# Variable-length attention: batches sorted by length on chip, and loops with one body per length class

## The chip, the cores and the metric

One Trainium2 chip, one of its cores. The traces show five engines, each with its own instructions, that work side by side (before the change PE is busy for 771.8 us of a span of 865.5, DVE for 562.0 and ACT for 549.9) and wait for one another: PE (TensorE, matrix multiply), DVE (VectorE), ACT (ScalarE), POOL (GpSimd) and SP (SyncE, which here issues most of the DMA transfers). The metric is the device time of one execution in microseconds. Executions of one kernel agree within about 1.3% here. A profiled execution gives a trace; "the span" is its length from first to last instruction, about 2 us less than the time.

## The reference

Self-attention over 32 batches of up to 512 rows, 8 heads of 64. Each batch has its own length between 64 and 511; rows from the length on are not attended to, and their output is zero.

```python
for b in range(32):
    n = lengths[b]
    q, k, v = split(x[b, :n] @ w_qkv)              # x is (32, 512, 512), w_qkv (512, 1536)
    scores = (q @ k.T) / 8                         # per head
    attn = softmax(scores)
    output[b, :n] = attn @ v                       # rows from n on stay zero
```

The draw is always the same. In classes of 64 rows (class c holds lengths up to 64c) there are, from class 8 down to class 2, 1, 3, 7, 5, 5, 6 and 5 batches. The mean length is about half of 512.

## The kernel before

The kernel before is straight-line code made by a tile framework: 32 times a projection stage (QK and V) followed by the attention stage of the batch before it. Lengths enter as masks only; every batch is computed at 512 rows.

```python
def stage_qkv(b):                                   # cut
    x16 = ...                                       # DVE: cast to f16
    for c in range(NC):                             # 16 PE transposes, ACT copies them out
        nc.tensor.transpose(pxt[:, t, :], x16[:, t, c*P:(c+1)*P], ident_f16)
        nc.scalar.copy(out=xT[:, c, :], in_=pxt)
    for m in range(2 * NC):                         # Q and K: 32 matmuls of 512 columns
        for c in range(NC):
            nc.tensor.matmul(pq, w_r[:, c, m*P:(m+1)*P], xT[:, c, :], ...)
        nc.vector.tensor_copy(out=qkT[:, m, :], in_=pq)
    for t in range(NT):                             # V: 16 matmuls of 512 columns
        ...
        nc.vector.tensor_scalar_mul(v_aug[:, t, :, 0:HD], pv, kmask[:, t, b:b+1])

def stage_attn(b):                                  # cut
    def emit_scores(i):                             # a pair of heads
        for kt in range(NT):
            psc = ps_s.tile([P, 2, MAXS], FP32)     # two such buffers in PSUM
            for par in range(2):                    # two heads, 64 rows each
                nc.tensor.matmul(psc[:, par, :], qkT[...], qkT[...])
            nc.scalar.activation(out=ep[:, :, kt, :], in_=psc, func=AF.Exp, scale=scale)
    def emit_av(i):
        ...                                         # 32 matmuls of 65 columns per pair, DVE divides
```

The softmax here doesn't subtract the row's maximum and nothing guards it: scores larger than these inputs give would overflow.

## Time and profile before

| | before |
|---|---|
| time, median of 8 runs (those beside the last experiments) | 867.6 us (865.5 to 868.9) |
| span of the profiled execution | 865.5 us |
| PE busy | 771.8 us, 89% |
| period of one batch | 26.0 us |

The first view is the profile's page: the line of busy times (share of the span, number of instructions), and the chain of work that ended last, as shares of the span.

```profile
PE 771.8 (89%) x7168; PEld 410.7 (47%) x7168; DVE 562.0 (65%) x1990; ACT 549.9 (64%) x645; POOL 1.1 (0%) x8
...
PE 53%; ACT 41%; issue 3%; DMA 1%; POOLq 0%; DVE 0%; ACTq 0%; POOL 0%
```

The second view is the costliest groups. The columns are line, engine, operation, tiles and shapes, count, then busy time and the mean of one in ns, then the engine's idle time just before them and what ended it.

```profile
L178 ACT ACTIVATE ep<-psc 128x1024 f16<-128x1024 f32 x512 | 482.1, 1068 | 281.6 <-PE psc L171 280.2
L171 PE MATMUL psc<-qkT 64*128 64x512 f16 x1024 | 230.0, 381 | 57.5 <-ACT ep L178 36.8
L127 PE MATMUL pq<-xT,w_r 128*128 128x512 f16 x1024 | 235.9, 384 | 6.4 <-ACT w_r L74 6.4
L188 PE MATMUL pav<-v_aug,ep 128*128 128x65 f16 x4096 | 206.2, 195 | 11.1 <-ACT ep L178 11.1
```

The third view is PE's timeline for part of one batch (start, duration, what, how many, and in brackets the idle time before).

```profile
300.10 6.86 PE L127 MATMUL pq<-xT,w_r 128*128 128x512 f16 x31
306.80 3.62 PE L141 MATMUL pv<-w_r,xT 128*128 128x512 f16 x16
310.35 0.61 PE L171 MATMUL psc<-qkT 64*128 64x512 f16 x4
310.89 0.69 PE L188 MATMUL pav<-v_aug,ep 128*128 128x65 f16 x17
311.92 0.39 PE L171 MATMUL psc<-qkT 64*128 64x512 f16 x2 [0.34 <-ACT ep L178]
```

Read them together. A batch has two phases: 10.3 us of projections that PE sets, in which ACT has nothing to do (its 281.6 us of idle time before exps), then about 15 us of attention in which ACT's 16 exps set the pace. Every batch takes the same 26.0 us, though half its rows are padding.

### The profile page before, as it was taken

To read this page: it belongs to the slowest core of one execution; us is meant where nothing else is said; L and a number is where in the kernel's file an instruction comes from. 1 tells how busy PE (TensorE), PEld (TensorE's weight loads), DVE (VectorE), ACT (ScalarE), POOL (GpSimd) and SP (SyncE) were. 2 spreads that over 40 slices of the span, in tenths; PEclk is the share of its full clock that TensorE was granted. 3 is DMA by queue.
4 is the path that set the end of the run, shared out by engine and by line. 5 is a ranking of instruction groups with operands and counts; after the bars stand their busy time and mean duration, and the time that the engine had idled before them with its cause. 6 is when DMAs were issued, how large, how long until landed. Compare 5 with 4: busy or idle time off the path is not lost.

```text
span 865.5 us, 17340 instructions
## 1 busy us (share of the span) xinstructions
PE 771.8 (89%) x7168; PEld 410.7 (47%) x7168; DVE 562.0 (65%) x1990; ACT 549.9 (64%) x645; POOL 1.1 (0%) x8
## 2 busy tenths in 40 slices
PE   2989999999999999999999999999999999998995
PEld 1344445454444444445444445444445444444453
DVE  2657666667666666666666666666766666765563
ACT  3186557766557766557756557756557756557756
POOL 0000000000000000000000000000000000000000
PEclk9899999999999999999999999999999999999999
DMA  9502322112222112332112223112222101111102
GB/s 335 199 1 98 98 98 98 54 45 98 99 98 99 53 46 98 98 99 98 51 48 99 98 98 99 50 50 98 99 98 99 49 3 50 50 49 51 40 11 98
DMA packets 34449, 71.37 MB, mean 82 GB/s; under 512 B 1090, under 2 KB 1090, under 8 KB 34370
## 3 DMA queue, kind: packets, MB, share of 16 engines
q1 hardware_dynamic: 34370, 70.26, 23.6%
q8 instruction: 56, 0.92, 0.4%
q14 instruction: 23, 0.19, 0.1%
HBM read 36.70 MB, written 33.55 MB: 81 GB/s over the span
## 4 chain that ended last, share of the span: by engine, by line
PE 53%; ACT 41%; issue 3%; DMA 1%; POOLq 0%; DVE 0%; ACTq 0%; POOL 0%
ACT ep L178 40%; PE pq L127 26%; PE pv L141 13%; PE psc L171 8%; PE pxt L117 4%; PE pav L188 2%; DMA w_f<-in_w_qkv_dram 1%; ACT w_r L74 0%; POOLq L259 0%; ACT xT L120 0%; ACTq L178 0%; ACTq L259 0%; DVE out_nat L205 0%; DVE iota_f L86 0%; DVE ident_f_95 L67 0%
## 5 line engine op out<-in xcount | busy, mean ns | idle before, releaser
L178 ACT ACTIVATE ep<-psc 128x1024 f16<-128x1024 f32 x512 | 482.1, 1068 | 281.6 <-PE psc L171 280.2
L171 PE MATMUL psc<-qkT 64*128 64x512 f16 x1024 | 230.0, 381 | 57.5 <-ACT ep L178 36.8
L127 PE MATMUL pq<-xT,w_r 128*128 128x512 f16 x1024 | 235.9, 384 | 6.4 <-ACT w_r L74 6.4
L188 PE MATMUL pav<-v_aug,ep 128*128 128x65 f16 x4096 | 206.2, 195 | 11.1 <-ACT ep L178 11.1
L134 DVE CAST qkT<-pq 128x512 f16<-128x512 f32 x256 | 173.9, 690 | 53.7 <-PE pq L127 53.5
L188 PEld LDWEIGHTS <-ep 128*128 128x128 f16 x4096 | 152.3, 97 | 116.2 <-issue 93.7
L127 PEld LDWEIGHTS <-w_r 128*128 128x128 f16 x1024 | 98.2, 99 | 127.0 <-issue 11.4
L171 PEld LDWEIGHTS <-qkT 64*128 64x128 f16 x1024 | 81.7, 93 | 96.5 <-issue 55.4
L141 PE MATMUL pv<-w_r,xT 128*128 128x512 f16 x512 | 115.7, 379 | 0.0
L148 DVE TENSOR_SCALAR v_aug<-pv,kmask 128x512 f16<-128x512 f32 x128 | 96.4, 753 | 16.0 <-PE pv L141 5.5
L120 ACT COPY xT<-pxt 128x512 f16<-128x512 f16 x128 | 67.6, 591 | 20.8 <-PE pxt L117 20.7
L141 PEld LDWEIGHTS <-xT 128*128 128x128 f16 x512 | 50.1, 98 | 60.4
L117 PE MATMUL pxt<-ident_f_95,x_129 128*128 128x128 f16 x16 | 1.9, 308 | 12.0 <-DVE ident_f_95 L67 12.0
L74 ACT CAST w_r<-w_f 128x1536 f16<-128x1536 f32 x4 | 5.9, 1480 | 4.8 <-DMA w_f<-in_w_qkv_dram 4.8
L117 PEld LDWEIGHTS <-x_129 128*128 128x128 f16 x16 | 1.7, 142 | 11.9 <-DVE x_129 L111 7.3
L153 DVE CAST v_aug<-kmask 128x32 f16<-128x32 f32 x32 | 7.0, 219 | 0.0
L111 DVE CAST x_129<-x_nat 128x2048 f16<-128x2048 f32 x1 | 1.2, 1227 | 6.0 <-DMA x_nat<-in_x_dram 6.0
L89 DVE TENSOR_TENSOR kmask<-iota_f,len_f 128x128 f32<-128x128 f32 x1 | 0.3, 293 | 4.7 <-POOL len_f L81 4.7
L86 DVE CAST iota_f<-iota_i 128x4 f32<-128x4 int32 x1 | 0.2, 247 | 4.2 <-POOL iota_i L84 4.2
L196 DVE TENSOR_SCALAR den_379<-pav,qbig 128x2 f32<-128x2 f32 x1 | 0.2, 219 | 4.1 <-PE pav L188 4.1
L111 DVE CAST x_6203<-x_nat 128x2048 f16<-128x2048 f32 x1 | 1.2, 1228 | 1.6 <-PE pxt L117 1.6
L111 DVE CAST x_8193<-x_nat 128x2048 f16<-128x2048 f32 x1 | 1.2, 1228 | 1.3 <-PE pxt L117 1.3
(1639 smaller groups left out, 447.5 us busy)
## 6 DMA issues: line engine op xcount, KB each, us to landing
x_nat<-in_x_dram SPq DMA_DIRECT2D x32, 1024.0 KB, 6.0
out_dram<-out_nat SPq DMA_DIRECT2D x32, 1024.0 KB, 5.2
w_f<-in_w_qkv_dram SPq DMA_DIRECT2D x4, 768.0 KB, 8.8
len_84<-in_lengths_dram SPq DMA_DIRECT2D x1, 0.2 KB
```

Source lines behind the costliest of these rows:

```text
L74: nc.scalar.copy(out=w_r[:, c, :], in_=w_f)
L111: nc.vector.tensor_copy(out=x16, in_=x_nat)
L117: nc.tensor.transpose(pxt[:, t, :], x16[:, t, c * P : (c + 1) * P], ident_f16)
L120: nc.scalar.copy(out=xT[:, c, :], in_=pxt.rearrange("p t q -> p (t q)"))
L127: nc.tensor.matmul(pq, w_r[:, c, m * P : (m + 1) * P], xT[:, c, :], start=(c == 0), stop=(c == NC - 1),)
L134: nc.vector.tensor_copy(out=qkT[:, m, :], in_=pq)
L141: nc.tensor.matmul(pv, xT[:, c, t * P : (t + 1) * P], w_r[:, c, 2 * D : 3 * D], start=(c == 0), stop=(c == NC - 1),)
L148: nc.vector.tensor_scalar_mul(v_aug[:, t, :, 0:HD], pv.rearrange("p (h d) -> p h d", d=HD), kmask[:, t, b : b + 1],)
L153: nc.vector.tensor_copy(out=v_aug[:, :, :, HD], in_=kmask[:, :, b].unsqueeze(2).broadcast_to([P, NT, NH]),)
L171: nc.tensor.matmul(psc[:, par, :], qkT[rq : rq + 64, NC + i, kt * P : (kt + 1) * P], qkT[rq : rq + 64, i, :], start=True, stop=True,)
L178: nc.scalar.activation(out=ep[:, :, kt, :], in_=psc, func=AF.Exp, scale=scale)
L188: nc.tensor.matmul(pav[:, par, :], ep[:, par, kt, qt * P : (qt + 1) * P], v_aug[:, kt, 2 * i + par, :], start=(kt == 0), stop=(kt == NT - 1),)
```

## The change

The intent is to do the work on valid rows only. The batches are ranked by length on DVE (comparisons and a permutation by a small matmul). Then every engine loops by itself: for each class from 8 down to 1 it has a body written for 64c rows, and it runs the body as often as a counter read from memory says. Buffers alternate by parity, so each class has an odd and an even body, and a first odd body in front ("peel") for an odd start. The x rows are cast to f16 by a DMA into a DRAM scratch and come back through a DMA transpose, so PE's transposes and ACT's copies of them go. Rows of the output past the last 128-row tile are written from a tile of zeros. Inside a body QK units of the next batch stand between the score units of the current one.

The core of the diff (some 900 lines in all; set-up, masks, semaphore bookkeeping and the old code are cut):

```diff
+class Shape:                                # one per class c
+        self.N = N = 64 * c
+        self.nk = nk = (c + 1) // 2          # tiles of 128 rows
+    def order(self):                         # one body: score units S, QK, AV and V
+        for p in range(4):                   # pairs of heads
+            while s_used < self.s_done(p):   # all score units of the pair in a row
+                out.append(("S", s_used))
+                s_used += 1
+            out += slots[p]                  # then the pair's share of QK
+            ...                              # then AV of the pair before
+    def run_loop(eng, name, block, regs, body, done):
+        for c in CLASSES:                    # 8 .. 1
+            with bb(L(c, 1, "in")):
+                eng.br_lt(r, 1, L(c, 1, "skip"), L(c, 1, "peel"))
+            with bb(L(c, 1, "peel")):
+                body(c, 1)
+                ...
+            with bb(L(c, 0, "body")):
+                body(c, 0)
+                eng.reg_add(r, r, -1)
+                eng.br_lt(r, 1, L(c, 0, "exit"), L(c, 1, "body"))
+            with bb(L(c, 1, "body")):
+                body(c, 1)
+                eng.reg_add(r, r, -1)
+                eng.br(L(c, 0, "in"))
+            ...
+    pS = nc.alloc_psum_tensor("pS", [P, 2, 2, 512], FP32)     # two score buffers
+    pQ = nc.alloc_psum_tensor("pQ", [P, 2, 512], FP32)
+    # POOL: per batch, mask copies, then x[perm[i]] -> f16 scratch by DMA
+    # SP, per batch:
+            ob = sp.value_load(perm[0:1, bass.ds(iv, 1)], min_val=0, max_val=B - 1)
+            sp.wait_ge(s_xfree, 1)
+            transpose(sp.snap(iv + 2, min_val=0, max_val=B + 1), 1 - p, n)
+            if nk < NT:
+                sp.dma_start(out=out[..., nk * P : MAXS, :], in_=zero[:, nk:NT, :])
+            sp.wait_ge(s_out[p], 1)
+            sp.dma_start(out=out[..., 0 : nk * P, :], in_=onat[1 - p][:, 0:nk, :])
```

## The prediction

> **What bounds it now.** The span is 865.5 us and strictly periodic: the chain of waits shows one 32-matmul QK block every 26.0 us, the same for every batch, whatever its length. Inside a period the timeline shows two phases. First QK+V: 6.8 + 3.5 us of back-to-back PE work while ACT idles 8.6 us (groups: ACT waits 280 us in all for scores). Then attention, paced by ACT: 16 exps of 128x1024, one per 0.92-0.94 us, about 15 us, with PE filling in scores and AV. The chain's shares say the same: PE 53%, ACT 41%. The start costs about 31 us until batch 0 is projected.
>
> **What the change removes.** Work on padding. For these 32 lengths the classes (rows/64) 8..2 hold 1, 3, 7, 5, 5, 6, 5 batches. Full-length matmul units, read from the timeline: a 512-column matmul 0.215 us, a score pair (two 64-row halves overlap) 0.27 us, an AV matmul 0.036 us. With c the class and nk = ceil(c/2), per batch: QK 0.86c, V 0.86nk, S 0.135·nk·c, AV 0.29·nk². Sums over the batches are 144, 79, 403, 221, so PE 124 + 68 + 54 + 64 = 310 us, against 19.2 x 32 = 614 us plus transposes (44 us busy, removed: a DMA transpose replaces them). ACT: exp cost about 0.09 us + 1 ns per 1.2 elements, 195 us in all instead of 482, and the 68 us of xT copies go. DVE: PSUM copies 0.15 us + N/0.96 ns (0.68 us at 512), V 0.75 us, an AV unit's add-reciprocal-multiply about 0.9-1.0 us because the three wait for each other: near 290 us. QK now sits between score bursts, so ACT no longer idles for a whole phase.
>
> **What it adds.** (1) Only two score buffers and bursts of 3-4 score units: PE waits for exp about 0.75 us per pair at classes 5-6, 1.7 us at 7-8. (2) DVE is as long as PE from class 4 down. (3) Loop chain: output issued, SP signals Pool, Pool copies the masks, PE's V waits for them, then DVE: about 7 us, more than the 3-4 us of work at class 2. (4) Taken branches.[...] No trace here shows it; I allow 25 us. (5) Start: sort of lengths, then cast copy in DRAM, then DMA transpose. I estimate 36 us before the loop.
>
> **Sum, per iteration** (PE or DVE plus stalls): class 8: 26; 7: 23.8; 6: 15.7; 5: 13.9; 4: 9; 3: 8; 2: 7. Weighted: 404 us. Plus 36 start, 25 branches, 5 tail: **470 us**, range 415 to 555. Nearly all of the removed work lies on the critical path, as the periodic chain shows.
>
> Chances: faster by over 2%: 0.98; within 2%: 0.01; slower: 0.01.
>
> **What would show it right.** PE busy about 320-350 us, about 70% of the span; ACT near 200, DVE near 300. The slices dense at first, thinner at the end. First QK matmul at 22-28 us. PE waits on exp near 70-90 us in all at the large classes; in the last 100 us PE waits for masks/xT (DMA or Pool).
>
> **What would make it wrong.** The DMA transpose or the DRAM-to-DRAM cast being slower than I take it[...]; at 10 us it would set the pace from class 5 down.[...]

The sum came to 470 us: 404 us for the iterations, 36 for the start, 25 for jumps and 5 for the tail.

The two formulas for costs by size were estimates: the trace before has one size of each (an exp 482.1 us / 512 = 942 ns at 1024 columns, a cast 690 ns at 512). The changed kernel's trace shows the sizes: exps of 640, 768, 896 and 1024 columns take 703, 811, 921 and 1026 ns (0.84 ns more per column, against 0.83 in the formula, which lies 80 to 84 ns below them), casts of 320, 384, 448 and 512 take 491, 558, 625 and 692 ns (1.05, against 1.04 in the formula, which lies 8 or 9 ns below).

## The result, and the profile after

The changed kernel takes 509.6 us (median of 4 runs, 506.8 to 511.7) against 867.8 us in the same round. The ratio is 0.587 (95% interval 0.584 to 0.590). Ratios in this document are the mean time of one kernel's fast runs over that of the other's of the same rounds, so not quite the ratio of the medians quoted. The prediction's 470 us was 8% too low; its range of 415 to 555 us holds the result.

The same lines of the page after, and the two lines of its DMA part that tell of instruction fetches (queue, packets, MB, share):

```profile
PE 368.1 (73%) x3791; PEld 210.0 (42%) x3791; DVE 288.6 (57%) x736; ACT 204.3 (40%) x262; POOL 43.4 (9%) x146
...
q8 instruction: 33, 0.54, 0.5%
q14 instruction: 59, 0.48, 0.3%
```

The groups after, the ones that answer to those above (all PE matmuls come from one helper line, so they are told apart by tile: pS are scores, pQ<-xT,w_r is QK, pA is AV):

```profile
L476 ACT ACTIVATE E<-pS 128x768 f16<-128x768 f32 (+3 forms) x257 | 200.7, 841 | 278.3 <-PE pS L283 278.2
L283 PE MATMUL pQ<-xT,w_r 128*128 128x384 f16 (+6 forms) x1056 | 167.3, 306 | 23.7 <-DMA xT<-x_f 13.9
L283 PE MATMUL pS<-qkT 64*128 64x384 f16 (+6 forms) x632 | 83.2, 316 | 91.3 <-ACT E L476 55.4
L283 PE MATMUL pA<-vaug,E 128*128 128x65 f16 x1768 | 74.4, 195 | 0.0
```

The exps fall from 482.1 to 200.7 us and PE's busy time from 771.8 to 368.1 us: the work has gone as forecast. But PE is now busy for only 73% of the span. The waits view names what it waits for before scores (us in total, times, longest):

```profile
PE pS L283 <- ACT E L476: 55.4, 80, 1.0
...
PE pS L283 <- issue: 19.8, 7, 3.6
PE pS L283 <- DMA xT<-x_f: 15.8, 10, 3.7
```

"Issue" means that no semaphore explains the gap. This is the surprise of the profile. The PE timeline at the entry to class 7 shows one:

```profile
62.72 1.14 PE L283 MATMUL pA<-vaug,E 128*128 128x65 f16 x32
67.44 0.61 PE L283 MATMUL pS<-qkT 64*128 64x448 f16 x4 [3.58 <-issue]
...
70.12 3.17 PE L283 MATMUL pQ<-xT,w_r 128*128 128x448 f16 x8
...
75.89 1.69 PE L283 MATMUL pQ<-xT,w_r 128*128 128x448 f16 x8
```

The DMA part of the page, asked for the 3.58 us of this gap alone (63.86 to 67.44 us), has one packet of an instruction queue in it:

```profile
q8 instruction: 1, 0.02, 2.1%
```

The trace keeps the start of every such packet. At each of the six long "issue" gaps before scores (2.9 to 3.6 us) one packet of 16 KB on q8 starts within 0.9 us of the start of the gap, and takes 1.0 to 1.5 us. So I take it that the engine had no instruction and that PE was waiting for a fetch. What fills the rest of the gap, the trace does not say. Two of the waits for the transposed input (at 367.6 and 482.5 us) have no such packet.

PE stands for 3.58 us, and then the first eight QK matmuls take 3.17 us; the next eight of the same shape take 1.69 us. So this entry costs twice: the gap, and some microseconds at half speed behind it. The windows view shows the granted clock there (the third number from the end; the other columns are named in experiment 1), and behind the gap of 2.94 us in class 4:

```profile
67.80:74.60 6.80, 5.33 (x19) 1.41 (x16) 1.25 (x2) 4.17 (x5) 0.49 (x1) 0.50 1.12 167
385.20:388.60 3.40, 3.40 (x27) 2.07 (x24) 1.85 (x5) 1.34 (x2) 0.49 (x1) 0.51 0.78 149
```

Behind each of the six long gaps the granted clock of the changed kernel goes to 0.50, within 0.1 to 2.1 us of the gap's end and for 3.4 to 13.7 us. It does not go by the length of the gap alone. The 2.94 us gap ends at 383.71 us; the first eight QK matmuls of 256 columns behind it still took 1.05 us, the next eight, from 385.38 us, 1.89 us. In the trace of experiment 5 a wait for the transposed input of 3.55 us (to 407.69 us) was followed by 32 QK matmuls of 128 columns in 1.96 us, no slower than the 32 behind a gap of 0.89 us (2.00 us). No limit comes out of these traces. In the changed kernel's loop the clock is halved for 44 us in all.

Each iteration's length can be read from the DVE memset that ends it. Before class 2, whose iterations vary from 4.9 to 8.3 us, seven iterations stand out from their class:

| class | its usual iteration | iterations that are longer | what PE waits for in them |
|---|---|---|---|
| 7 | 24.2 us | 29.6, 28.7 | issue 3.6 and 3.0 us |
| 6 | 16.8 | 23.7 | issue 3.2 and 2.0 us |
| 5 | 15.8 to 16.4 | 23.2 | issue 3.1 us |
| 4 | 8.8 | 13.5, 12.4 | transposed x 3.7 us; issue 2.9 us |
| 3 | 8.3 | 11.8 | issue 3.5 us |

In class 5 even the usual iteration is long, and there the gap is on DVE. DVE's timeline (the memset ends the iteration before; the casts are the first work of the next):

```profile
327.42 0.06 DVE L595 MEMSET scr<- 128x1 f32 x1
...
330.56 0.89 DVE L540 CAST qkT<-pQ 128x320 f16<-128x320 f32 x2 [3.08 <-issue]
```

This returns in each of the last three class 5 iterations (9.0 us of DVE waits for "issue" in all).

The order in which the built program's instructions stand gives the reason that I then tested: the even body ends in a test whose first target is the exit, and the program lays the exit right behind it (seen in the list of blocks of the built program, which no view here shows). The odd bodies of all classes stand behind everything else, at the end of the program. So the step from even to odd body is a far jump over the bodies of all later classes; a single class 6 body is 280 instructions on PE (140 matmuls, each with its weight load). An entry at the even parity jumps over the peel body as well.

### The profile page after: what moved, and what is told of

Read it like the earlier page. It is cut to its first block, busy times and chain, and to the rows that moved or that the text cites. A ratio compares the mean times of both kernels' runs of the same rounds, so it can differ in the third digit from the quotient of the medians.

```text
span 504.9 us, 10568 instructions
## 1 busy us (share of the span) xinstructions
PE 368.1 (73%) x3791; PEld 210.0 (42%) x3791; DVE 288.6 (57%) x736; ACT 204.3 (40%) x262; POOL 43.4 (9%) x146
## 5 line engine op out<-in xcount | busy, mean ns | idle before, releaser
L476 ACT ACTIVATE E<-pS 128x768 f16<-128x768 f32 (+3 forms) x257 | 200.7, 841 | 278.3 <-PE pS L283 278.2
L540 DVE CAST qkT<-pQ 128x384 f16<-128x384 f32 (+3 forms) x190 | 110.8, 585 | 174.7 <-PE pQ L283 160.0
L283 PE MATMUL pQ<-xT,w_r 128*128 128x384 f16 (+6 forms) x1056 | 167.3, 306 | 23.7 <-DMA xT<-x_f 13.9
L283 PE MATMUL pS<-qkT 64*128 64x384 f16 (+6 forms) x632 | 83.2, 316 | 91.3 <-ACT E L476 55.4
L283 PEld LDWEIGHTS pQ<-xT,w_r 128*128 128x128 f16 x1056 | 89.9, 102 | 83.4 <-issue 44.4
L283 PE MATMUL pQ<-w_r,xT 128*128 128x512 f16 x332 | 80.9, 382 | 0.9 <-DVE vaug L548 0.8
L283 PEld LDWEIGHTS pS<-qkT 64*128 64x128 f16 x632 | 23.2, 94 | 137.5 <-ACT E L476 67.1
L283 PEld LDWEIGHTS pA<-vaug,E 128*128 128x128 f16 x1768 | 70.2, 99 | 15.0 <-issue 0.5
L283 PE MATMUL pA<-vaug,E 128*128 128x65 f16 x1768 | 74.4, 195 | 0.0
L585 DVE TENSOR_TENSOR onat<-pA,rcp 128x256 f32<-128x256 f32 (+1 forms) x134 | 63.3, 472 | 6.5
L548 DVE TENSOR_SCALAR vaug<-pQ,kcur 128x512 f16<-128x512 f32 x83 | 61.4, 749 | 9.4 <-PE pQ L283 7.6
L283 PEld LDWEIGHTS pQ<-w_r,xT 128*128 128x128 f16 x332 | 28.7, 98 | 37.7 <-DVE vaug L548 9.6
L620 POOL DMA_DIRECT2D x_f<-in_x_dram x35 | 17.2, 492 | 59.1 <-issue 47.7
```

Of the source, the lines that this page charges most:

```text
L283: m = te.matmul(o, l, r, start=start, stop=stop)
L476: m = se.activation(out=o, in_=src, func=AF.Exp, scale=scale)
L540: m = ve.tensor_copy(out=qkT[p][:, js[0] : js[-1] + 1, 0:n], in_=pQ[:, u % 2, 0 : n * len(js)].rearrange("p (j n) -> p j n", n=n),)
L548: m = ve.tensor_scalar_mul(vaug[p][:, t, :, 0:HD], pQ[:, k % 2, :].rearrange("p (h d) -> p h d", d=HD), kcur[p][:, t : t + 1],)
L585: m = ve.tensor_tensor(out=o[:, qts[0] : qts[-1] + 1, pairs[0] * P : (pairs[-1] + 1) * P].rearrange("p q (h d) -> p q h d", d=HD), in0=src ...
L620: pe.dma_start(out=xs[bass.ds(iv, 1), 0:n, :].rearrange("o s d -> (o s) d"), in_=x[bass.ds(b, 1), 0:n, :].rearrange("o s d -> (o s) d"),). ...
```

## The experiments

All times are medians; "before" was run again with each group (867.2 to 868.8 us).

### 1. No jumps at all

The loop is replaced by its straight-line expansion for these 32 lengths. The kernel is right for this draw only; it is a probe.

```diff
-        top = nc.cur_bb ... all blocks and branches of run_loop
+        for i, c in enumerate(SCHED):        # [8] + [7]*3 + [6]*7 + [5]*5 + [4]*5 + [3]*6 + [2]*5
+            body(c, 1 - i % 2)
+        done()
```

> The same bodies in the same order for these 32 lengths, laid out in a straight line, without loops, counters or jumps. Theory A (a taken jump to instructions that are not yet fetched stalls the engine about 3 us, and PE then runs slowly for some us): the six slow iterations on PE (29.6, 28.7, 23.7, 23.2, 12.4, 11.8 us against 24.2, 16.8, 15.8, 8.8, 8.3 of their neighbours, about 32 us together) and the 3.1 us DVE stalls in three iterations of class 5 go; about 470 to 480 us. Rival B (those iterations are slow from late transposes, DMA contention or the granted clock): within 1% of 509.6 us.

Measured: 461.3 us (460.4 to 461.9), ratio to before 0.5312 against 0.5871. The jumps cost 48 us, more than the 30 to 40 us that I had counted. The windows view shows it class by class. Columns: stretch, its length, then busy time (and instructions) of PE, weight loads, DVE, ACT and POOL, the granted clock, the DMA share, GB/s. First the changed kernel, classes 8 to 2 in order:

```profile
37.70:65.30 27.60, 20.17 (x210) 9.81 (x208) 14.54 (x38) 15.08 (x16) 0.00 (x0) 1.00 0.15 21
65.30:147.70 82.40, 61.05 (x630) 30.46 (x630) 39.66 (x111) 41.22 (x50) 3.21 (x12) 0.94 0.33 75
147.70:272.10 124.40, 97.43 (x980) 51.85 (x979) 71.47 (x169) 61.68 (x84) 7.25 (x28) 0.97 0.41 107
272.10:360.20 88.10, 69.00 (x710) 39.74 (x712) 48.35 (x121) 38.64 (x61) 5.18 (x20) 0.92 0.41 99
360.20:412.40 52.20, 43.25 (x435) 27.84 (x436) 34.12 (x95) 19.57 (x20) 4.99 (x20) 0.93 0.70 156
412.40:465.80 53.40, 45.47 (x549) 31.94 (x547) 38.21 (x115) 20.31 (x25) 5.99 (x24) 0.97 0.57 165
465.80:495.80 30.00, 18.44 (x239) 13.91 (x236) 17.31 (x50) 4.17 (x5) 4.82 (x20) 0.94 0.69 201
```

Then the straight-line kernel, the same classes:

```profile
37.70:65.20 27.50, 20.64 (x214) 9.90 (x212) 14.48 (x38) 16.09 (x18) 0.00 (x0) 1.00 0.10 21
65.20:137.50 72.30, 56.50 (x626) 29.54 (x626) 39.81 (x112) 40.19 (x49) 3.20 (x12) 1.00 0.36 83
137.50:254.80 117.30, 95.64 (x983) 51.48 (x982) 71.44 (x169) 62.12 (x85) 7.23 (x28) 1.00 0.47 113
254.80:331.10 76.30, 63.01 (x709) 37.32 (x710) 48.62 (x121) 37.88 (x60) 5.17 (x20) 1.00 0.48 113
331.10:375.40 44.30, 40.69 (x443) 26.90 (x444) 34.11 (x95) 20.27 (x20) 4.98 (x20) 1.00 0.78 185
375.40:424.90 49.50, 43.27 (x540) 30.14 (x541) 38.20 (x115) 19.56 (x24) 5.96 (x24) 1.00 0.74 177
424.90:453.00 28.10, 18.93 (x240) 14.61 (x237) 17.18 (x50) 4.22 (x5) 4.80 (x20) 0.94 0.79 216
```

The work is the same (DVE 263.65 and 263.85 us over the seven stretches). The loop takes 415.3 us instead of 458.1. The excess is 10.1 us in class 7, 7.1 in class 6, 11.8 in class 5, 7.9, 3.9 and 1.9 in classes 4 to 2. The granted clock returns to 1.00 in all classes but the last, and PE's busy time falls by 16 us with no matmul removed. Even the 3.7 us wait for the transposed input in the second class 4 iteration is gone here; but a 2.9 us wait at the same place comes back in experiment 5 without the far jumps, and goes in experiment 9, so it is not shown that the jumps made it. Every class 5 iteration is 15.3 us now: of each 3 us gap on DVE only about 1.0 us had reached the iteration's length. Theory A holds (its 470 to 480 us was too high), B falls.

### 2. All batches as class 8

> The class thresholds are all set to zero, so all 32 batches run as class 8 (512 rows), results stay right. Theory C (the whole gain is the skipped padding; the new structure is no faster per full row): start 37.7 us plus 32 iterations of about 27.5 us (the one class-8 iteration took 27.6) plus 9 us, about 925 us, slower than before. Rival D (a good part of the gain is the DMA transpose and the interleaving of QK with scores): below 800 us.

```diff
-        pe.iota(thr[:, :], pattern=[[64, 8]], base=0, ...)     # class thresholds
+        pe.iota(thr[:, :], pattern=[[0, 8]], base=0, ...)      # every length counts as class 8
-            sp.wait_ge(s_z, zc)                                # no zeros are written now
```

Measured: 919.3 us, ratio to before 1.060. The skipped padding is worth 919.3 - 509.6 = 410 us, all of the gain and more. The 6% is not in the steady work, though: an iteration takes 26.1 us, against 26.0 in the kernel before. Of the 47.7 us between the spans (913.2 and 865.5) some 37 us lie in start and end (38.1 + 32.7 = 70.8 us, against 865.5 - 32 x 26.0 = 33.5). After the last iteration (880.5 us) the span runs on for 32.7 us. From 886 us on, when the last output has landed, no engine works and the only packets are instruction fetches (9 on q8, 7 on q14): the loops have only the seven empty classes to pass.

PE waits before scores for exps 183.0 us in all, in 256 waits; that is the price of the score bursts, which experiment 3 takes up (there the class 8 iteration falls from 27.6 to 23.1 us). Theory C holds, but its 925 us came that near partly by luck: 32 iterations took 842 us and not 880, the end 32.7 us and not 9.

### 3. Score units one at a time

In classes 5 to 8 a QK or AV unit follows each score unit from the second on. The order in classes 1 to 4 is unchanged.

```diff
+    def order_fine(self):                    # used where a body has 12 or 16 score units
+        for j in range(ns):
+            out.append(("S", j))
+            if j == 0: continue
+            # an AV unit whose exps are done (its pair's last S was 3 units ago), if the last was QK,
+            # otherwise the next QK unit
+            ...
```

For class 6 the body becomes S0 S1 QK0 S2 QK1 S3 QK2 S4 QK3 S5 AV0 S6 QK4 ... in place of S0 S1 S2 QK0 QK1 S3 S4 S5 QK2 QK3 AV0 ....

> In classes 5 to 8 the score units no longer come in bursts of 3 or 4: after every score unit from the second on, one QK or AV unit follows. Theory E (PE waits for exp only because two score buffers are filled in a burst; 5.1 us per class 7 iteration, 3.1 us in class 6, 2.8 us in class 5, about 57 us in all): PE's waits for ACT fall by at least 40 us and the time by 40 to 50 us, to 460 to 470 us. Rival F (DVE, or ACT itself, is as long as PE there, so the wait turns up elsewhere): at most 15 us less, above 494 us.

Measured: 482.6 us (479.0 to 484.7), ratio 0.5543: 27 us less, where E expected 40 to 50 and F at most 15. The waits themselves went as E says: PE's waits before score matmuls for exps fall from 55.4 to 0.2 us, and a class 6 iteration takes 14.7 us instead of 16.8. PE's timeline in class 6, first of the changed kernel (three score units and two QK units in a row, with the gap for the second buffer):

```profile
196.63 0.50 PE L283 MATMUL pS<-qkT 64*128 64x384 f16 x4
197.88 0.34 PE L283 MATMUL pS<-qkT 64*128 64x384 f16 x2 [0.74 <-ACT E L476]
198.15 1.47 PE L283 MATMUL pQ<-xT,w_r 128*128 128x384 f16 x8
```

and interleaved:

```profile
190.02 0.34 PE L312 MATMUL pS<-qkT 64*128 64x384 f16 x2
190.29 0.82 PE L312 MATMUL pQ<-xT,w_r 128*128 128x384 f16 x4
191.05 0.34 PE L312 MATMUL pS<-qkT 64*128 64x384 f16 x2
191.32 0.72 PE L312 MATMUL pA<-vaug,E 128*128 128x65 f16 x18
```

Most of the missing part went to jumps: PE's "issue" waits before scores rose from 19.8 to 26.2 us, DVE's from 9.0 to 14.0 us, and three class 5 iterations take 17.4 to 18.8 us in this kernel. Neither expectation was met as written; experiments 5 and 6 settle it.

### 4. The odd body next to the even one

One line: the test that closes the even body is turned round, so that the odd body is the target laid next to it.

```diff
-                eng.br_lt(r, 1, L(c, 0, "exit"), L(c, 1, "body"))
+                eng.br_ne(r, 0, L(c, 1, "body"), L(c, 0, "exit"))
```

> Only the test that closes the even body is turned round (jump to the odd body if the counter is not zero, instead of jump to the exit if it is below one), so that the odd body lies next to the even body in the program instead of behind all the others. Theory A (distance decides[...]): the 3 us stalls at the first entry to the odd bodies go, 20 to 35 us less, 475 to 490 us. Rival G (any taken jump costs it, near or far): no change, within 1% of 509.6 us.

Measured: 476.5 us (475.6 to 479.6), ratio 0.5478: 33 us less by one line, and the kernel stays general. Every class 6 iteration is 16.7 to 16.9 us and the class 5 loop runs at 15.3 us; DVE's waits for "issue" before these casts are down from 9.0 to 1.1 us. PE's timeline at the second class 7 iteration, the first that enters the odd body (in the changed kernel PE stood for 2.98 us at this place):

```profile
94.92 1.14 PE L283 MATMUL pA<-vaug,E 128*128 128x65 f16 x32
95.99 0.55 PE L283 MATMUL pS<-qkT 64*128 64x448 f16 x4
```

Two PE gaps are left, of 3.5 and 3.6 us, in the first iterations of classes 7 and 5 (30.7 and 20.4 us against 24.1 and 15.3). Both enter at the even body and so jump over the peel body. (Classes 3 and 2 do that too, without a gap; their bodies are shorter.) Theory A's forecast holds and G falls. But distance is not the whole of it. In the changed kernel PE goes on between the even and the far odd body of class 6 for four more iterations of 16.7 to 16.9 us, without a gap. The first jump back has a packet on q8 (203.5 us). From 205 to 271 us, over the next three jumps, the only instruction queue with packets is q14:

```profile
q14 instruction: 10, 0.08, 0.4%
```

So what cost PE there was the first entry to a far body (3.18 and 2.04 us of gaps in class 6); a far jump back to a body that it had run before cost nothing. Bodies laid one behind the other cost no gap either: the straight-line kernel has 30 packets on q8 and none of these gaps. In experiment 4 the step to the odd body may be no taken jump at all any more, so this run alone does not tell a near jump from none. DVE is different: in class 5 of the changed kernel it stands about 3 us in each of the last three iterations, with a packet on q14 starting in each of these gaps (312.1, 328.8 and 344.8 us).

### 5 and 6. Interleaving with adjacent bodies, and without jumps

> The finer interleaving and the adjacent odd bodies together. Theory (the two losses are separate: jumps cost 33 us in the adjacent-bodies run, score bursts 57 us of waits of which the interleaving run got 27 us back because its jump stalls grew): the interleaving is worth 35 to 45 us once the jumps are cheap, 432 to 442 us; class 6 iterations 14.7 us, class 5 about 13 to 14 us. Rival (the interleaved bodies are held by something else, so gains don't add): about 450 us or more.

Measured: 438.1 us (436.9 to 442.5), ratio 0.5038. With cheap jumps the interleaving is worth 476.5 - 438.1 = 38 us, as expected; class 6 at 14.6 to 14.8 us, class 5 at 13.5 to 13.7 (18.3 in its first iteration, which still jumps over the peel body). This version is general and beats both kernels.

> The finer interleaving in a straight line, no jumps at all: the floor for this structure at these lengths. From the unrolled run's 461.3 us less 2.1 us in each of 7 class 6 iterations, 1.5 to 2 us in 5 of class 5, 4 us in 4 of classes 7 and 8: 415 to 425 us, if the interleaving is really worth about 40 us; about 435 us if the interleaving run's 27 us was all.

Measured: 420.8 us, ratio 0.4852, in the middle of the 415 to 425 forecast. Without jumps the interleaving is worth 461.3 - 420.8 = 40.5 us. Experiment 3 fell 13 us short of this with the far jumps in place; without them the shortfall is gone, so it was theirs (the waits named there add up to 11 us).

### 7. No writes of zeros

Adjacent bodies, and the block of the SP body that writes the zeros is deleted. Padded rows are then never written and the result is wrong (the comparison gives nan).

> Adjacent odd bodies, and the writes of zeros to the padded output rows are left out (the result may be wrong, on purpose). Theory H (in classes 2 to 4 the transposes come late because they share the DMA engines and the issuing queue with up to 0.75 MB of zeros per batch): PE's 13.6 us of waits for the transposed input shrink to a few us, the 9.5 and 6.6 us iterations of class 2 become 5 us, 7 to 12 us less than the adjacent-bodies run's 476.5 us. Rival I (the chain load, cast, transpose, output itself is longer than a class 2 iteration, whatever else is moved): less than 3 us changes.

Measured: 473.3 us, ratio 0.5459 (0.5438 to 0.5481) against 0.5478 (0.5468 to 0.5487) with the zeros. The medians are 3 us apart, the ratios less than 2 us, and their intervals overlap: the difference is not clear of the noise. PE's waits before scores for the transposed input fall from 13.6 to 8.8 us, in classes 3 and 4. The slow iterations of class 2 stay (9.1 and 6.7 us; 9.5 and 6.6 with the zeros). H falls: the 7 to 12 us are not there. I's "less than 3 us" fits, though its reason is not shown by this run; experiment 9 takes it up.

### 8. Prefetch hints

Interleaving and adjacent bodies; PE and DVE carry a prefetch hint for the closing jump at the top of both looped bodies.

```diff
             with bb(L(c, 0, "body")):
+                loc = eng.mark_branch_hint_location()
                 body(c, 0)
                 eng.reg_add(r, r, -1)
-                eng.br_ne(r, 0, L(c, 1, "body"), L(c, 0, "exit"))
+                eng.br_ne(r, 0, L(c, 1, "body"), L(c, 0, "exit")).branch_hint(loc)
```

> As the interleaving with adjacent bodies, and PE and DVE put a prefetch hint for the closing jump at the top of each looped body. If the stalls left (entries of a class that skip its first body, 3 to 4 us each, some five of them) are not at the hinted jumps, the hints gain nothing: within 1% of the run without them. If jumps between the two bodies still stall, several us less.

Measured: 454.5 us (453.0 to 457.8), ratio 0.5233: 16 us slower than without hints, which neither sentence allowed for. PE's "issue" waits before scores go from 6.9 to 22.9 us; gaps of 2.8 to 4.4 us come back at the first odd bodies of classes 7 and 6 and at the entries of classes 3 and 2, where the version without hints had none. In each of these four gaps a 16 KB packet starts on q8 (86.6, 162.2, 361.1 and 416.1 us), so I take them for waits for fetches again. Why the hint brings them back is open; no run here separates it.

### 9. SyncE's bookkeeping off the chain

What holds class 2 is a chain over two iterations, read in the trace of experiment 5: 0.3 us from the end of an iteration to the output issue, 2.1 us from there to the next transpose issue (SP loads and adds registers), 3.7 to 4.1 us until the transpose has landed, and then the iteration that uses it (5.3 us from the score matmul that waits for it to its end): an estimate of about 11.5 us for two iterations, against 2 x 4.9 us for the fastest iteration seen. The load of the output's place is not needed before the transpose.

```diff
-            ob = sp.value_load(perm[0:1, bass.ds(iv, 1)], min_val=0, max_val=B - 1)
-            sp.reg_add(it, it, 1)
             ...
             transpose(sp.snap(iv + 2, min_val=0, max_val=B + 1), 1 - p, n)
+            ob = sp.value_load(perm[0:1, bass.ds(iv, 1)], min_val=0, max_val=B - 1)
+            sp.reg_add(it, it, 1)
```

> Interleaving and adjacent odd bodies, and in the SyncE body the load of the batch's place for the output moves from before the next transpose to after it. Theory J (classes 2 to 4 wait for the transposed input because a chain over two iterations, output issue, about 2 us of SyncE bookkeeping, 3.6 us transpose, 5.3 us iteration, is longer than two iterations of PE work): about 1 us comes off the chain, class 2 iterations average 5.5 us or less instead of 6.1, PE's 17.1 us of waits for the transposed input shrink by 5 us or more, time 431 to 435 us, ratio about 0.498. Rival K (the transposes' own time on the DMA engines decides): no change, ratio 0.5038.

Measured: 428.7 us (426.2 to 431.2), ratio 0.4939 (0.4919 to 0.4959) against 0.5038. SP's timeline, first of experiment 5 (output issue at 413.22, next transpose 2.09 us later):

```profile
413.22 0.34 SPq L730 DMA_DIRECT2D out_dram<-onat  x1
415.31 1.23 SPq L703 DMA_TRANSPOSE xT<-x_f  x1
```

and of experiment 9 (0.93 us later):

```profile
412.33 0.34 SPq L730 DMA_DIRECT2D out_dram<-onat  x1
413.26 1.23 SPq L703 DMA_TRANSPOSE xT<-x_f  x1
```

PE's waits before scores for the transposed input fall from 17.1 us to:

```profile
PE pS L312 <- DMA xT<-x_f: 5.1, 3, 2.9
```

The class 4 stragglers (12.6 and 9.7 us in experiment 5) are back at 8.8, and class 2 averages 5.4 us instead of 6.1. K's "no change" falls, and J's forecast is met or passed: the gain of 9 us is more than its 3 to 7. But the edit did a second thing. The write of zeros now comes 2.1 us behind the transpose instead of 1.4, and the transposes land sooner: their median from issue to landing falls from 6.6 to 3.5 us in class 4, from 4.9 to 3.0 in class 3 and from 3.9 to 2.8 in class 2. So the transposes' own time has a part in the gain beside the 1.2 us of bookkeeping; no run separates the two. This is the fastest general version found: 2.02 times as fast as the kernel before, in 16% less time than the changed one.

| kernel | median us | ratio to before | general |
|---|---|---|---|
| the change | 509.6 | 0.5871 | yes |
| 1 straight line | 461.3 | 0.5312 | no |
| 2 all as class 8 | 919.3 | 1.0604 | yes |
| 3 interleaved | 482.6 | 0.5543 | yes |
| 4 adjacent bodies | 476.5 | 0.5478 | yes |
| 5 both | 438.1 | 0.5038 | yes |
| 6 interleaved, straight line | 420.8 | 0.4852 | no |
| 7 adjacent, no zeros | 473.3 | 0.5459 | wrong result |
| 8 as 5, with hints | 454.5 | 0.5233 | yes |
| 9 as 5, SP order | 428.7 | 0.4939 | yes |

## Why the prediction was right, point by point

The direction and the range were right; 470 us was low by 40. The sum, beside what the profiled execution (span 504.9 us) showed:

| term | predicted | measured | read from |
|---|---|---|---|
| start, until the first scores | 36 us | 37.7 | timeline |
| 32 iterations without jump costs | 404 | 415.3 | straight-line run, windows |
| jumps in the loop | 25 | 42.8 | the changed kernel's loop less that |
| tail | 5 | 9.1 | timeline |

- "Nearly all of the removed work lies on the critical path": right. With nothing skipped the new kernel takes 919.3 us.
- "QK now sits between score bursts, so ACT no longer idles for a whole phase": true, but it bought nothing by itself. At full length an iteration takes 26.1 us, as long as the old period of 26.0 (experiment 2), because the bursts make PE wait.
- "(1) PE waits for exp about 0.75 us per pair at classes 5-6, 1.7 us at 7-8": the mechanism was right, and in class 6 so was the size (3.1 us per iteration for four pairs). In class 7 it is 5.1 us per iteration, not 6.8. It was worth removing: 38 to 40 us (experiments 5 and 6). The forecast of 70 to 90 us of such waits compares with 55.4 us in the waits of PE's score matmuls.
- "(2) DVE is as long as PE from class 4 down": not quite. In the straight-line run DVE is busy for 84 to 91% of PE's time in classes 4 to 2.
- "(3) Loop chain ... about 7 us": a chain longer than the work does hold class 2, but the mask is not its last link (2.8 us of PE waits in all). Its last link is the transposed input. Class 2 averaged 6.0 us.
- "(4) Taken branches ... I allow 25 us": the term that was mis-sized most, an allowance that no trace had shown. The runs show 42.8 us in the profiled pair and 48 us between medians. Missing from the prediction's account were the slow matmuls behind each gap, DVE's own gaps in class 5, and that all odd bodies lie at the end of the program. In class 6 PE paid at the first entry to a body only, not on every iteration (experiment 4).
- "(5) Start ... 36 us", "First QK matmul at 22-28 us": 37.7 and 23.9 us.
- "PE busy about 320-350 us, ACT near 200, DVE near 300": 368.1, 204.3 and 288.6 us. Most of PE's excess goes with the jumps: 352.0 us in the straight-line run, at a mean granted clock of 0.99 instead of 0.949.
- The iterations: class 8 26 forecast and 27.6 measured, 7 23.8 and 24.1, 6 15.7 and 16.7, 5 13.9 and 15.3, 4 9 and 8.8, 3 8 and 8.2 (straight-line run for classes 7 and down). Classes 5 and 6 alone make 14 us of the shortfall (7 x 1.0 and 5 x 1.4). Class 2 hides half of that: 7 forecast and 5.6 measured, 7 us too many over its five iterations.
- The transpose: The changed kernel's took 3.4 to 9.0 us from issue to landing (median 4.5): the two of 0.52 MB at the start 5.2 and 4.5, the five of 0.13 MB in class 2 3.4 to 4.4, so a quarter of the bytes took hardly less time. They set no class's pace above class 2 in the straight-line run: every iteration there has its class's usual length to within 0.3 us.

## What to carry to other kernels

Skipping padding on chip paid here (509.6 against 867.8 us) even with a loop of its own on every engine, but part of the loop's price was set by where the bodies lie in the built program, not in the source (33 us, mended by one line): look for engine gaps that no semaphore explains (2.9 to 3.6 us here), and lay the bodies that follow each other next to each other before trying anything subtler. With two buffers between PE and ACT, put other PE work after every unit that fills one, not after a burst (38 us here). And when two faults overlap, the gain of mending one is measured only once the other is mended: here the interleaving gave 27 us alone and 38 us behind the other fix.
